# Decoder layer on one core: two of the seven products of the down-projection accumulated onto PSUM banks that were read before, and the first output rows finished by accumulating stores

## The chip, the core and the metric

The kernel runs on one core of a Trainium2 chip. Its engines are TensorE (PE, matrix products into eight banks of PSUM), VectorE (DVE), ScalarE (ACT), GpSimd (POOL) and SyncE (SP, which here only issues DMAs). PEld is the part of PE that loads the stationary operand of a matmul. The metric is the device time of one launch in microseconds (us); lower is better.

## The reference, cut to what matters

One decoder layer on a sequence of 512 tokens and 1024 channels in float32: two attention branches and their projections, then a gated MLP with a causal convolution of width 3. The attention part is not touched. The last lines are what the change works on:

```python
x = _layer_norm(DEEPNORM_ALPHA * x + (1.0 + gt1) * attn_out, ln1_g, ln1_b)
u2 = x * (1.0 + sc2) + sh2
h = _causal_depthwise_conv(u2 @ w_up, conv_w, conv_b)      # 1024 -> 2 x 2816
h_gate, h_val = jnp.split(h, 2, axis=-1)
ffn_out = (jax.nn.silu(h_gate) * h_val) @ w_down           # 2816 -> 1024
x = _layer_norm(DEEPNORM_ALPHA * x + (1.0 + gt2) * ffn_out, ln2_g, ln2_b)
```

`_layer_norm` subtracts the mean of a row, multiplies by the reciprocal of its standard deviation, multiplies by the row `ln2_g` and adds the row `ln2_b` (the offset row).

## The kernel before, in words

**Three matmuls for one product.** A float32 product is made of three matmuls on halves of reduced precision: high times high, high times low, low times high. Each weight that is loaded is therefore split: ACT copies it into the high half (`wh` or `wdh`, L182 for most), DVE subtracts that from the loaded weight (`wl` or `wdl`, L91). For activations the two halves lie in one tile `hv` (or `fh` and `fo`), 256 columns each.

**Loads.** SP issues the weight loads in a fixed order, that of a list of items (`add_item`, L956 to 1025). An item is a load into one of five raw buffers (`raw`, `LOADS = 5`) and the work on it, such as the split into one of three buffers (`WBUFS = 3`). `weights(k)` fetches item k and works off the ones before it. On PE, DVE, ACT and POOL the order of the program is only a wish: a scheduler places the instructions of each engine, which then run in the order that it set.

**Up-projection** (L1099 to 1145). 44 tiles of 128 hidden channels (n = 0 to 43), each of 24 matmuls into one PSUM bank, then convolution on ACT and DVE, SiLU on ACT, and the gate product on DVE. Two tiles make one of 22 gated tiles; two of these, `e` and `o`, make one of the 11 pairs (`FP = 11`, p = 0 to 10) of the down-projection.

**Down-projection.** For a pair, the 512 tokens are halved into rows blocks 0 and 1 above, 2 and 3 below, and the 1024 output columns into a left and a right half. So a pair is a product of 2 x 2 blocks with the weight blocks b11, b12, b21, b22 (128x512 each, stored in `wdp[p]` in the order b11, b12, b22, b21). It is done with seven block products in place of eight, each of them summed over the 11 pairs into two PSUM banks, one for each of its two row blocks:

- P1 (with b11), Y and Z2 run inside the up-projection and hold six banks (`yz`; `early_products`, L1087), for the last pair inside phase z.
- Z is phase z, with T3, a combination of two weight blocks; W1 is phase v, with T1, another one; X is phase x, with b21 as it is; W is phase w, with b22.

`blocks` (L1050) makes the combinations of activations (`g`, `s4`, and the changed `e`) on DVE. For the weights, `add_pair_items` loads b11 and b12 and adds b12 and b22 to them with an accumulating load of POOL, which gives the tile `b` with T1 in its left and T3 in its right half. `pair_proc` (L940 to 957) makes the two weights of Y and Z2 from b22 (L946) and b21 (L947), splits them, and stores `b` to a scratch tensor `t13[p]` and b22, multiplied by the gate row, to `wgt[p]`. The phases z, v and w load these again. The last pair (p = 10) has no such detour for `b`: it is split at once (`state["t13"]`).

**The gate row.** The channel gate multiplies the columns of the result (`g0` for the left, `g1` for the right half, both in `gt[1]`). In before, W alone has it in its weights (b22 is multiplied ahead); the other products are multiplied as results, in `gated` (L1155), one multiplication and one addition of 128x512 on DVE into the residual tile `r[i][e]` (row block i, half e; `xn` in the trace).

**The tail.** Phase x ends the row blocks 0 and 1: `first_rows` (L1226) makes their statistics and then `tail` (L1163): mean step (L1169), scaling and offset (L1173), store. Phase w has three pairs' weights loaded in its turn and the last eight (`LATE = 8`, `cli`) loaded early. For these eight, row block 2 is done in one piece of 512 columns into W's first bank and row block 3 in two pieces of 256 columns into fresh banks; then come subtraction or addition into `r`, statistics, `ln_stats` (L852) and `tail`, whose stores SP issues.

## Time and profile before

| what | value |
|---|---|
| three timed runs | 755.17, 755.78, 755.90 us, median 755.78 |
| the profiled execution | 754.3 us |
| its span (first to last instruction) | 752.5 us |
| granted clock of PE, mean | 0.995 |
| busy: PE, DVE, ACT, POOL | 98%, 81%, 51%, 14% of the span |
| read from and written to memory | 117.07 MB, 10.22 MB |

The profile is of one execution on the chip. A row of its timeline has the start of a group of alike instructions in us from the start of the span, the busy time of the group, the engine, the line of the program, the operation, what it writes and reads, and the count; in brackets, where the engine had stood idle before, how long, and which engine's work ended the wait. A row of the views of waits has the waiting engine and line, the work that released it, then the sum of the waits, their count and the longest.

### The profile page before, as it was taken

Reading aid. Unit: us, or ns where it says so; the run is one execution under the profiler, and the core shown is the slowest. Engines: PE = TensorE matmul, PEld = TensorE weight load, DVE = VectorE, ACT = ScalarE, POOL = GpSimd, SP = SyncE. Lnnn points to the kernel's source line nnn. Section 1 sums busy time; section 2 is a strip of 40 time slices with the busy share of each in tenths; the row PEclk is TensorE's granted clock in tenths of the full one; section 3 lists DMA queues with packets and bytes.
Section 4 is the critical chain, followed back from the end, with each engine's and each line's share of the span. In section 5 each row is a group of like instructions: output and inputs, shape, how many; then the busy total and the mean of one; then the engine's idle time right before and its main releaser. Section 6 shows DMA issues by size and latency. Waiting matters only on the chain.

```text
span 752.5 us, 9875 instructions
## 1 busy us (share of the span) xinstructions
PE 734.0 (98%) x3478; PEld 607.6 (81%) x3478; DVE 607.1 (81%) x1017; ACT 386.0 (51%) x678; POOL 109.0 (14%) x138
## 2 busy tenths in 40 slices
PE   8999999999999999999999999999999999999993
PEld 4878888878888888788889888888888888887883
DVE  6869799888788894765587889987696678769997
ACT  4566566685866564433065554454454355346530
POOL 1026223453010011453000000000000000000010
PEclk9999999999999999999999999999999999999997
DMA  8943446313422331542063778587874665557611
GB/s 331 405 175 116 164 169 214 122 58 112 169 92 83 108 112 62 195 168 84 1 240 77 252 243 275 161 250 223 253 213 165 187 218 151 171 182 264 220 63 57
DMA packets 43252, 128.01 MB, mean 170 GB/s; under 512 B 5665, under 2 KB 6177, under 8 KB 43202
## 3 DMA queue, kind: packets, MB, share of 16 engines
q1 hardware_dynamic: 37602, 112.09, 42.5%
q0 software_dynamic: 2576, 7.41, 5.2%
q10 hardware_dynamic: 3024, 7.88, 3.0%
q8 instruction: 27, 0.44, 0.2%
q14 instruction: 23, 0.19, 0.1%
HBM read 117.07 MB, written 10.22 MB: 169 GB/s over the span
## 4 chain that ended last, share of the span: by engine, by line
PE 82%; DVE 10%; DMA 3%; issue 2%; ACT 2%; POOL 0%; SPq 0%; DVEq 0%; ACTq 0%
PE ps L135 18%; PE ps L133 18%; PE ps L134 18%; PE ps L301 5%; PE ps L1077 3%; PE ps L1078 2%; PE ps L1076 2%; PE ps L552 2%; DVE wl L91 2%; PE ps L534 2%; PE ps L893 2%; PE ps L892 2%; PE ps L894 2%; PE ps L475 1%; PE ps L476 1%
## 5 line engine op out<-in xcount | busy, mean ns | idle before, releaser
L91 DVE TENSOR_TENSOR wl<-raw,wh 128x1024 fp32r<-128x1024 f32 (+2 forms) x112 | 139.2, 1244 | 53.9 <-ACT wh L182 53.5
L182 ACT ACTIVATE wh<-raw 128x1024 fp32r<-128x1024 f32 (+1 forms) x103 | 108.5, 1053 | 124.0 <-PE ps L134 59.8
L133 PE MATMUL ps<-u2h,wh 128*128 128x512 f32 (+1 forms) x376 | 141.6, 377 | 0.0
L135 PE MATMUL ps<-u2h,wl 128*128 128x512 f32 (+1 forms) x376 | 141.2, 376 | 0.0
L134 PE MATMUL ps<-u2l,wh 128*128 128x512 f32 (+1 forms) x376 | 141.2, 376 | 0.0
L133 PEld LDWEIGHTS ps<-u2h,wh 128*128 128x128 f32 x376 | 70.8, 188 | 13.6 <-issue 0.8
L135 PEld LDWEIGHTS ps<-u2h,wl 128*128 128x128 f32 x376 | 70.8, 188 | 12.8
L134 PEld LDWEIGHTS ps<-u2l,wh 128*128 128x128 f32 x376 | 70.8, 188 | 12.7
L133 PE MATMUL ps<-uh,wh 128*128 128x512 f32 x200 | 79.4, 397 | 0.0
L135 PE MATMUL ps<-uh,wl 128*128 128x512 f32 x200 | 78.3, 391 | 0.9 <-DVE wl L91 0.9
L134 PE MATMUL ps<-ul,wh 128*128 128x512 f32 x200 | 78.3, 391 | 0.0
L1124 ACT ACTIVATE cv<-ps,cw 128x512 f32<-128x512 f32 x44 | 33.9, 770 | 24.9 <-PE ps L135 19.0
L135 PEld LDWEIGHTS ps<-uh,wl 128*128 128x128 f32 x200 | 37.6, 188 | 9.5 <-DVE wl L91 1.3
L161 POOL DMA_DIRECT2D raw<-in_wdp x11 | 9.5, 867 | 244.1 <-DVE raw L947 95.0
L514 POOL TENSOR_TENSOR pt<-pt,om 128x127 f32<-128x127 f32 (+3 forms) x32 | 43.2, 1360 | 8.0 <-DVE om L513 8.0
L133 PEld LDWEIGHTS ps<-uh,wh 128*128 128x128 f32 x200 | 37.6, 188 | 7.4
L134 PEld LDWEIGHTS ps<-ul,wh 128*128 128x128 f32 x200 | 37.6, 188 | 7.2
L1125 DVE SCALAR_TENSOR_TENSOR cv<-ps,cw,cv 128x511 f32<-128x511 f32 x44 | 32.8, 745 | 9.1 <-ACT cv L1124 9.1
L1132 ACT ACTIVATE cv<-cv 128x512 f32<-128x512 f32 x22 | 13.9, 630 | 39.0 <-DVE cv L1126 38.9
L1126 DVE SCALAR_TENSOR_TENSOR cv<-ps,cw,cv 128x510 f32<-128x510 f32 x44 | 32.8, 745 | 0.2
L633 POOL TENSOR_TENSOR raw<-raw,gt 128x1024 f32<-128x1024 f32 x8 | 20.9, 2618 | 66.9 <-DMA raw<-in_wo 54.4
L513 DVE TENSOR_TENSOR_SCAN om<-om,dg 128x127 f32<-128x127 f32 (+3 forms) x32 | 29.6, 982 | 0.5 <-ACT om L508 0.4
(226 smaller groups left out, 1607.3 us busy)
## 6 DMA issues: line engine op xcount, KB each, us to landing
raw<-in_wup SPq DMA_DIRECT2D x44, 512.0 KB, 4.6
raw<-in_wa SPq DMA_DIRECT2D x32, 512.0 KB, 4.3
raw<-in_wct SPq DMA_DIRECT2D x25, 512.0 KB, 3.7
raw<-in_wdp SPq DMA_DIRECT2D x22, 512.0 KB, 5.7
wa<-in_wa SPq DMA_DIRECT2D x14, 512.0 KB, 7.9
raw<-in_wdp SPq DMA_DIRECT2D x22, 256.0 KB, 4.6
raw<-in_wdp POOLq DMA_DIRECT2D x11, 512.0 KB, 7.7
t<-raw ACTq DMA_DIRECT2D x10, 512.0 KB, 3.6
```

Of the source, the lines that this page charges most:

```text
L91: state["read"] = V.tensor_tensor(o, i, fl(hi), ALU.subtract)
L133: PE.matmul(ps, wh, ah, start=first, stop=False)
L134: PE.matmul(ps, wh, al, start=False, stop=False)
L135: return PE.matmul(ps, wl, ah, start=False, stop=last)
L182: state["hi"] = S.activation(h[:, 0:cols], r[:, 0:cols], AF.Copy)
L301: PE.matmul(grp[g], w, u, start=j == 0 and n == 0, stop=j == KT - 1 and n == (1 if g == 7 else 2))
L513: V.tensor_tensor_scan(d0, d0, dg[:, 513 - (e - s) : 512][:, ::-1], 0.0, ALU.mult, ALU.max)
L514: G.tensor_tensor(pt[b][:, s : e - 1], pt[b][:, s : e - 1], om[:, s + 1 : e], ALU.mult)
L1077: PE.matmul(ps, ah, bl, start=False, stop=False)
L1124: S.activation(t, ps, AF.Identity, bias=cw[:, n, 3:4], scale=cw[:, n, 2:3])
L1125: V.scalar_tensor_tensor(t[:, 1:], ps[:, 0:511], cw[:, n, 1:2], t[:, 1:], ALU.mult, ALU.add)
L1126: V.scalar_tensor_tensor(t[:, 2:], ps[:, 0:510], cw[:, n, 0:1], t[:, 2:], ALU.mult, ALU.add)
```

## The change

Seven things are changed, which hang together.

1. **T1 is multiplied by the gate row ahead** (`g1`, columns 512 to 1023 of `gt[1]`). For pairs 2 to 10, `pair_proc` does it on DVE before `b` is stored or split. For pairs 0 and 1, whose `b` is stored too early for that, two new items at up-tiles 23 and 27 load the T1 half of `t13[p]`, multiply it and store it back on POOL's queue (`scale_proc`).
2. **s4 changes its sign.** With it W1 + W, as gated sums, can be made by subtraction alone.
3. **X goes onto P1's two banks and W onto W1's two banks.** `product` and `phase` get a switch for it: the first matmul does not start the bank anew. No banks are taken for X and W, except the two 256-column pieces of row block 3 as before. P1 is read by DVE (through ACT's copy `p1`) before X begins; a bank of W1 is read before W's first matmul on it.
4. **The results are folded into `r` in another order.** Before: the four sums are built first and each is multiplied and added as a whole (`gated`). After: Y's, Z's and Z2's parts are folded as soon as they exist (`z_mark` 4 and 5, `v_mark` 2 to 5), W1 goes into `r[0][1]` and `r[1][1]` by one subtraction each (`x_mark`), P1 with X on it is multiplied straight from PSUM (`w_mark`), and W1 with W on it is subtracted at the end.
5. **The tail of row blocks 0 and 1 moves** with its statistics to `x_mark` 3 and 4 (`ROWS = (3, 4)`), the same phase steps as before, but each behind its subtraction of W1.
6. **Their output is filled ahead with the offset row:** two stores of 512 KB (128 rows each) from `lnr2[1]` on ACT's queue at up-tiles 30 and 32.
7. **They are finished by accumulating stores:** the mean step is done on DVE, the scaling with the row's reciprocal deviation on ACT in place of DVE's scaling and addition, and POOL issues the store with `accum_op=ALU.add`, which adds to what lies in the output.

The diff, cut to its core:

```diff
+ROWS = (3, 4)
...
             w = wdc_proc(r)
+            if p > 1:
+                V.tensor_tensor(b[:, 0:512], b[:, 0:512], gt[1][:, 512:1024], ALU.mult)
             with tc.issue_after(state["last"].ins):
...
+        if n in (23, 27):
+            t = t13[(23, 27).index(n)][:, 0:512]
+            add_item(t, scale_proc(t), 512)
...
-        V.tensor_tensor(s4, o[:, hi], e[:, lo], ALU.subtract)
+        V.tensor_tensor(s4, e[:, lo], o[:, hi], ALU.subtract)
...
+        if n in (30, 32):
+            S.dma_start(out[(n - 30) * 64 : (n - 30) * 64 + P, :], lnr2[1])
...
-                    product(ps[i], t[:, top[i]], t[:, bot[i]], *half(w, a), p == 0, p == FP - 1)
+                    product(ps[i], t[:, top[i]], t[:, bot[i]], *half(w, a), fresh and p == 0, p == FP - 1, not fresh)
...
             for i in range(2):
                 V.tensor_tensor(u2[i], p1[i], Y[i], ALU.subtract)
-                V.tensor_tensor(q1[i], u2[i], Z2[i], ALU.add)
+        if n in (4, 5):
+            fold(n - 2, 1, tm[n - 4], u2[n - 4], ALU.subtract)
...
-        if n == 0:
-            for i in range(2):
-                V.tensor_tensor(q1[i], q1[i], Z[i], ALU.add)
-                V.tensor_tensor(u3[i], u2[i], Z[i], ALU.add)
-        if n in (1, 2):
-            gated(n - 1, 0, q1[n - 1], q1[n - 1])
+        if n in (0, 1):
+            for a, b, c in zip((u3, q1)[n], (u2, u3)[n], (Z, Z2)[n]):
+                V.tensor_tensor(a, b, c, ALU.add)
+        if n in (2, 3):
+            fold(n - 2, 0, q1[n - 2], q1[n - 2])
+        if n in (4, 5):
+            fold(n - 4, 1, u3[n - 4], u3[n - 4], ALU.subtract)
...
-        tail(i, st, [(0, 0, 512), (1, 0, 512)], G)
+        tb = slice(i * P, (i + 1) * P)
+        mu, rs = ln_stats(st[:, 0:2, :])
+        for e in range(2):
+            c, v = slice(e * 512, (e + 1) * 512), r[i][e]
+            V.scalar_tensor_tensor(v, v, mu, lnr[0][:, c], ALU.subtract, ALU.mult)
+            S.activation(v, v, AF.Copy, scale=rs)
+            G.dma_start(out[tb, c], v, accum_op=ALU.add)
 
     def x_mark(n):
-        if n == 0:
-            for i in range(2):
-                V.tensor_tensor(c22[i], u3[i], W1[i], ALU.add)
-                V.tensor_tensor(u2[i], u2[i], W1[i], ALU.add)
-        if n in (1, 2):
-            gated(n - 1, 1, c22[n - 1], c22[n - 1], ALU.subtract)
-        if n in (3, 4):
-            first_rows(n - 3)
-        if n == 4:
-            for i in range(2):
-                gated(2 + i, 1, u2[i], u2[i], ALU.subtract)
-
+        if n in ROWS:
+            i = ROWS.index(n)
+            V.tensor_tensor(r[i][1], r[i][1], W1[i], ALU.subtract)
+            first_rows(i)
...
-    X = [bank() for _ in range(2)]
-    phase(X, xi, FP, lambda p: ops[p][1], x_mark)
-    W = [bank() for _ in range(2)]
+    phase(P1, xi, FP, lambda p: ops[p][1], x_mark, fresh=False)
...
-                V.tensor_tensor(p1[i], p1[i], X[i], ALU.add)
-                gated(2 + i, 0, p1[i], p1[i])
+                fold(2 + i, 0, p1[i], P1[i])
...
-                product(W[i], t[:, top[i]], t[:, bot[i]], *half(w, a), p == 0, i == 1 and p == FP - LATE - 1)
+                product(W1[i], t[:, top[i]], t[:, bot[i]], *half(w, a), False, i == 1 and p == FP - LATE - 1, True)
...
-    V.tensor_tensor(r[3][1], r[3][1], W[1], ALU.add)
+    V.tensor_tensor(r[3][1], r[3][1], W1[1], ALU.subtract)
...
-            V.tensor_tensor(v, v, ps, ALU.add)
+            V.tensor_tensor(v, v, ps, ALU.subtract)
```

The scheduler's order moves at three places. In the rows stand the line, the operation, the tile written and the tiles read (with buffer numbers), and the shape. The lines of after are six higher in the region of the product and one or some higher elsewhere.

On DVE, at the pair step of the last pair (p = 10, before L946 to 957): `raw_6255` (after: `raw_6273`) is the loaded b22 and b21, `raw_6217` (after: `raw_6235`) the tile `b` with T1 and T3, `gt_4554` the gate row, `wl` the low half of a weight of phase z, `hv` an activation's low half. Before:

```order
L946 TENSOR_TENSOR raw_6255<-raw_6255,raw_6217 128x512
L91 TENSOR_TENSOR wl_6460<-raw_6386,wh_6459 128x1024
L947 TENSOR_TENSOR raw_6255<-raw_6255 128x512
L91 TENSOR_TENSOR wdl_6371<-raw_6255,wdh_6369 128x512
L91 TENSOR_TENSOR wl_6490<-raw_6419,wh_6489 128x1024
L91 TENSOR_TENSOR wdl_6372<-raw_6255,wdh_6370 128x512
L91 TENSOR_TENSOR wdl_6380<-raw_6217,wdh_6378 128x512
L91 TENSOR_TENSOR wdl_6381<-raw_6217,wdh_6379 128x512
```

After:

```order
L947 TENSOR_TENSOR raw_6273<-raw_6273,raw_6235 128x512
L92 TENSOR_TENSOR wl_6479<-raw_6405,wh_6478 128x1024
L948 TENSOR_TENSOR raw_6273<-raw_6273 128x512
L92 TENSOR_TENSOR wdl_6389<-raw_6273,wdh_6387 128x512
L951 TENSOR_TENSOR raw_6235<-raw_6235,gt_4554 128x512
L92 TENSOR_TENSOR wdl_6390<-raw_6273,wdh_6388 128x512
L92 TENSOR_TENSOR wl_6507<-raw_6438,wh_6506 128x1024
L92 TENSOR_TENSOR wdl_6399<-raw_6235,wdh_6397 128x512
L92 TENSOR_TENSOR wdl_6400<-raw_6235,wdh_6398 128x512
L92 TENSOR_TENSOR hv_6432<-cv_6162,hv_6432 128x256
```

The scaling of T1 (L951) stands where a 1024-wide `wl` stood, and that `wl` comes one place later, behind the second `wdl`.

On PE, at the end of phase x and the start of phase w: `ps_6643` is a bank of X, `ps_6826` and `ps_6827` are W's banks for row blocks 2 and 3, `ps_6896` is the first 256-column piece of row block 3, `wl_6813` the low half of phase w's first weight. Before, the rows behind the last ones shown here are the other matmuls of the two 256-column pieces; the first 512-column low matmul comes when all 48 of them are done:

```order
L1078 MATMUL ps_6643<-wh_6776,hv_6416 128x512
L1076 MATMUL ps_6826<-wh_6812,hv_4191 128x512
L1076 MATMUL ps_6827<-wh_6812,hv_4191 128x512
L1076 MATMUL ps_6896<-wdh_6544,hv_4902 128x256
L1077 MATMUL ps_6896<-wdl_6545,hv_4902 128x256
L1078 MATMUL ps_6896<-wdh_6544,hv_4902 128x256
L1076 MATMUL ps_6896<-wdh_6588,hv_5128 128x256
```

After, `ps_4308` is a bank of P1, `ps_6538` and `ps_6539` are W1's banks, `ps_6905` is the 256-column piece and `wl_6826` the low half of phase w's first weight:

```order
L1084 MATMUL ps_4308<-wh_6792,hv_6435 128x512
L1082 MATMUL ps_6538<-wh_6825,hv_4191 128x512
L1082 MATMUL ps_6539<-wh_6825,hv_4191 128x512
L1082 MATMUL ps_6905<-wdh_6563,hv_4904 128x256
L1083 MATMUL ps_6905<-wdl_6564,hv_4904 128x256
L1084 MATMUL ps_6905<-wdh_6563,hv_4904 128x256
L1083 MATMUL ps_6538<-wl_6826,hv_4191 128x512
L1084 MATMUL ps_6538<-wh_6825,hv_4191 128x512
L1083 MATMUL ps_6539<-wl_6826,hv_4191 128x512
```

Three 256-column matmuls stand ahead of the first low one in place of 48; the other 45 now come last on PE, behind all of row block 2.

On DVE, from the end of row block 2 on: `xn_3625` and `xn_3626` are the two halves of row block 2, `xn_3742` is the right half of row block 3, `mv` the statistics, `ln_0` and `ln_1` the rows of the layer norm. Before:

```order
L1279 TENSOR_TENSOR xn_3742<-xn_3742,ps_6896 128x256
L1279 TENSOR_TENSOR xn_3742<-xn_3742,ps_6923 128x256
L1280 BN_STATS st_6829<-xn_3742 128x6 x2
L1279 TENSOR_TENSOR xn_3626<-xn_3626,ps_6826 128x512
L1280 BN_STATS st_6828<-xn_3626 128x6
L854 BN_AGGR mv_6883<-st_6828 128x2
L854 BN_AGGR mv_6950<-st_6829 128x2
```

After:

```order
L1284 TENSOR_TENSOR xn_3626<-xn_3626,ps_6538 128x512
...
L1284 TENSOR_TENSOR xn_3742<-xn_3742,ps_6905 128x256
L861 SCALAR_TENSOR_TENSOR mv_6892<-mv_6892 128x1
L1285 BN_STATS st_6840<-xn_3742 128x6
L1180 SCALAR_TENSOR_TENSOR xn_3625<-xn_3625,mv_6892,ln_1_5281 128x512
L1180 SCALAR_TENSOR_TENSOR xn_3626<-xn_3626,mv_6892,ln_1_5281 128x512
L1284 TENSOR_TENSOR xn_3742<-xn_3742,ps_6932 128x256
L1285 BN_STATS st_6840<-xn_3742 128x6
```

Row block 2 is now subtracted first and scaled (L1180) ahead of the last piece of row block 3; before, row block 3's right half was added first and both tails stood behind row block 2's last subtraction.

26 lines of the change are left out of this document (13 added, 13 removed).

## The prediction, on record before the result

> **What bounds the kernel now.** I read the page first: the share of each engine and the chain that ended last.
>
> ```profile
> span 752.5 us, 9875 instructions
> ...
> PE 734.0 (98%) x3478; PEld 607.6 (81%) x3478; DVE 607.1 (81%) x1017; ACT 386.0 (51%) x678; POOL 109.0 (14%) x138
> ...
> PE 82%; DVE 10%; DMA 3%; issue 2%; ACT 2%; POOL 0%; SPq 0%; DVEq 0%; ACTq 0%
> ```
>
> TensorE (PE) is busy nearly all the time, so a change that takes no matmul away can gain only where PE waits or where it has ended. The view by windows, cut at the stages that the change touches, shows where that is.
>
> ```profile
> core 0: us, PE busy (x) PEld busy (x) DVE busy (x) ACT busy (x) POOL busy (x), PEclk, DMA share, GB/s
> 560.00:665.00 105.00, 105.00 (x465) 86.92 (x464) 76.88 (x124) 45.99 (x75) 3.45 (x4) 1.00 0.62 187
> ...
> 681.00:692.00 11.00, 10.66 (x45) 7.91 (x44) 10.89 (x18) 7.95 (x16) 0.00 (x0) 1.00 0.66 221
> 692.00:724.50 32.50, 32.50 (x145) 26.92 (x144) 31.79 (x52) 17.89 (x26) 0.00 (x0) 1.00 0.52 177
> 724.50:741.00 16.50, 15.60 (x91) 13.51 (x89) 15.24 (x30) 0.29 (x1) 2.23 (x4) 1.00 0.17 64
> 741.00:752.50 11.50, 0.15 (x1) 0.00 (x0) 7.92 (x22) 0.48 (x2) 0.00 (x0) 0.65 0.25 92
> ```
>
> Up to 665 PE never rests and VectorE (DVE) has a quarter of its time free. From 681 on DVE is full (10.89 of 11.00, then 31.79 of 32.50). The last 11.5 us have no matmul: DVE finishes rows 2 and 3, then the output lands. PE's waits after 400 us, and ScalarE's (ACT) wait in the up-projection, are these rows of the views of waits:
>
> ```profile
> PEld ps L1077 <- DVE wdl L91: 1.2, 2, 0.7
> PEld ps L1077 <- DVE wl L91: 1.1, 1, 1.1
> ```
>
> ```profile
> ACT wh L182 <- PE ps L134: 33.0, 14, 5.0
> ```
>
> The 1.2 us lie in the last early products (687 to 690), the 1.1 us at the first split weight of phase w (731). ACT waits 14 times, up to 5.0 us, for PE to free a weight buffer: through the up-projection the weights are ahead of PE.
>
> **The up-projection: nothing.** Eleven DVE operations of 0.69 us are added (nine scalings of T1 in the pair step, two of the reloaded tiles), two 256 KB loads on SP's queue, two 256 KB stores on POOL's, two 512 KB stores of the offset row on ACT's. What hides them is the quarter of DVE that is free and the buffers that wait for PE. In the order each is placed beside work that waits already: the SP load of the first tile needs a slot that an early product before up-tile 19 frees, some eight tiles of the stream ahead; ACT's first fill stands behind the copy that waits for the layer-norm row today. If that cover were gone, a late weight costs PE its lateness beyond the reserve, up to 5.0 us. I take 0; the ends are 0 and 1 us.
>
> **The last pair product: +0.6 us.** Here DVE is full and PE waits for it. These are DVE's rows, then PE's weight loads.
>
> ```profile
> 687.00 0.68 DVE L91 TENSOR_TENSOR wdl<-raw,wdh 128x512 fp32r<-128x512 f32 x1
> 687.61 1.22 DVE L91 TENSOR_TENSOR wl<-raw,wh 128x1024 fp32r<-128x1024 f32 x1
> 688.74 1.89 DVE L91 TENSOR_TENSOR wdl<-raw,wdh 128x512 fp32r<-128x512 f32 x3
> 690.55 0.75 DVE L91 TENSOR_TENSOR hv<-cv,hv 128x256 fp32r<-128x256 f32 x2
> ```
>
> ```profile
> 689.48 0.19 PEld L1077 LDWEIGHTS ps<-wdl,fh 128*128 128x128 f32 x1 [0.52 <-DVE wdl L91]
> ...
> 691.02 0.19 PEld L1078 LDWEIGHTS ps<-wdh,hv 128*128 128x128 f32 x1
> ```
>
> The first fence of the section on the change shows the new scaling between the first and the second `wdl`, in place of a 1024-wide `wl`, which goes behind. Three 512-wide operations in a row take 1.89, so one occupies 0.60 of the queue and the `wl` 1.13 (687.61 to 688.74). The second `wdl` therefore starts at 688.21 and not 688.74, and PE loses its 0.52 us wait. But the `hv` at 690.55 gets later by the added 0.60, and PE stands at its low half already today (690.97 against the load at 691.02). So PE leaves this place 0.60 later; the earlier half microsecond is given back. Ends: 0 if the low half is not what holds it, 1.2 if ACT's splits, which now wait for the scaling, add as much again.
>
> **Phases z, v and x: DVE work, no time by itself.** From the first `u2` to the last fold the old order has 45 operations of 512 columns, the new one 35: six additions go because B21's products land on P1's banks and B22's on W1's, and four scalings go to ACT, which stands idle for 18 us at the end:
>
> ```profile
> 742.94 0.48 ACT L856 ACTIVATE mv<-mv,epsc 128x1 f32<-128x1 f32 x2 [18.15 <-DVE mv L854]
> ```
>
> PE does as many matmuls as before, with the same loads; that the first of a product accumulates too costs nothing by itself, since today the second and third do and PE shows no gap between them (145 matmuls fill 32.50 us, 0.224 each). PE is solid from 692 to 724.5, so all of this counts only where DVE meets PE again.
>
> **Phase w: -1.1 us and a new order.** PE's rows now, and the DVE and ACT rows that set its wait:
>
> ```profile
> 724.30 0.41 PEld L1076 LDWEIGHTS ps<-wh,hv 128*128 128x128 f32 x2
> ...
> 724.98 0.19 PEld L1077 LDWEIGHTS ps<-wdl,hv 128*128 128x128 f32 x1
> ...
> 730.49 0.19 PEld L1078 LDWEIGHTS ps<-wdh,hv 128*128 128x128 f32 x1
> 731.78 0.19 PEld L1077 LDWEIGHTS ps<-wl,hv 128*128 128x128 f32 x1 [1.10 <-DVE wl L91]
> ...
> 740.54 0.19 PEld L1078 LDWEIGHTS ps<-wdh,hv 128*128 128x128 f32 x1
> ```
>
> ```profile
> 715.20 1.06 ACT L182 ACTIVATE wh<-raw 128x1024 fp32r<-128x1024 f32 x1 [1.14 <-PE ps L1078]
> ```
>
> ```profile
> 719.03 1.28 DVE L1229 BATCH_NORM_STATS2 st<-xn 128x6 f32<-128x512 f32 x2
> ...
> 722.88 0.69 DVE L1229 BATCH_NORM_STATS2 st<-xn 128x6 f32<-128x512 f32 x1
> ...
> 730.51 1.22 DVE L91 TENSOR_TENSOR wl<-raw,wh 128x1024 fp32r<-128x1024 f32 x1
> ```
>
> Today PE does the 48 matmuls of 256 columns (row block 3) first, 0.12 us each (46 steps in 5.51 us), because the `wl` of phase w stands behind 11.5 us of DVE work (719.03 to 730.51); it still waits 1.10 us, then does the 512-wide ones, 0.225 each. After, 45 of the 48 come last. When is `wl` there? DVE's work for rows 0 begins behind the split of x's fifth weight, which ACT starts at 715.20 when PE frees a buffer, so at 715.80 with the 0.60 from above; 1.06 on ACT and 1.13 on DVE bring it to 718.1. Ahead of `wl` then stand two subtractions of W1, four statistics, two short splits (eight times 0.60), two mean steps of 0.66 and some 0.5 us of small ones: 6.6 us, so `wl` runs from 724.7 to 725.9. PE ends x at 724.90, has two hi matmuls (0.45) and three small ones (0.36) and wants `wl` at 725.7. It waits about 0.15 us; ends 0 and 1.1. PE's last load: 740.54 + 0.60 - 1.10 + 0.15 = 740.2.
>
> A new wait goes with the banks: PE's first matmul onto W1 of rows 1 must wait for DVE's subtraction from that bank, on which the rest of PE's queue then hangs. In the sum above the subtraction ends at 723.3, and today's statistics of rows 1 start at 722.88; PE wants the bank at 725.1, so 1.8 us are in hand and I take 0. On this the Trainium skill, Perfetto Trace Analysis, section Optimizing Tensor Performance, has a rule against the change: independent matmul groups should rotate through PSUM banks, so that an evacuation overlaps the next group. By the rows the sum gets 0 from it; by the rule PE would stand for the evacuation. No run so far shows the case; it is the slower rival below.
>
> **After the last matmul: -3.5 us.** DVE's rows, SP's stores, and the price of 256-wide operations:
>
> ```profile
> 738.36 0.75 DVE L1279 TENSOR_TENSOR xn<-xn,ps 128x256 f32<-128x256 f32 x2
> 739.02 0.75 DVE L1280 BATCH_NORM_STATS2 st<-xn 128x6 f32<-128x256 f32 x2
> 741.19 0.69 DVE L1279 TENSOR_TENSOR xn<-xn,ps 128x512 f32<-128x512 f32 x1 [1.42 <-PE ps L1078]
> ...
> 742.64 0.31 DVE L854 BATCH_NORM_AGGREGATE mv<-st 128x2 f32<-128x12 f32 x2
> ...
> 744.46 0.15 DVE L857 TENSOR_SCALAR mv<-mv 128x1 f32<-128x1 f32 x1
> ...
> 744.66 0.75 DVE L1169 SCALAR_TENSOR_TENSOR xn<-xn,mv,ln 128x512 f32<-128x512 f32 x1
> 745.32 1.41 DVE L1173 SCALAR_TENSOR_TENSOR xn<-xn,mv,ln 128x512 f32<-128x512 f32 x2
> ...
> 747.64 1.54 DVE L1173 SCALAR_TENSOR_TENSOR xn<-xn,mv,ln 128x512 f32<-128x512 f32 x3
> ```
>
> ```profile
> 746.10 3.62 SPq L1174 DMA_DIRECT2D out<-xn  x5
> ```
>
> Today both row blocks' tails stand behind PE: 741.19 to 749.18, 8.0 us. After, rows 2 end first on PE and their tail lies beside the 45 small matmuls. For rows 3 alone remain: half of 0.75 to subtract, half of 0.75 for statistics, 0.24 to aggregate, 744.66 to 749.18 without the two scalings of rows 2 (4.52 - 1.33 = 3.2), and 0.3 for a reciprocal and the gaps between dependent ones: 4.5 us. Does the tail of rows 2 fit? Its last matmul loads 45 times 0.12 before 740.2, at 734.8; DVE starts 0.65 later (as 740.54 to 741.19), needs 3.27 (741.19 to 744.46), then 0.75 for the first half of rows 3 and 1.33 to scale: 740.8. The last piece is there at 740.2 + 0.55 = 740.75. It just fits, without reserve. DVE ends at 740.75 + 4.5 = 745.25, against 749.18. The last store takes what it takes today, 3.3 us to 752.5.
>
> The accumulating stores of rows 0 and 1 are new. DVE and ACT have rows 1 ready at about 729. What such a store takes lies between these two rows, the plain store and the accumulating load of twice the size:
>
> ```profile
> out<-xn POOLq DMA_DIRECT2D x4, 256.0 KB, 2.4
> ...
> raw<-in_wdp POOLq DMA_DIRECT2D x11, 512.0 KB, 7.7
> ```
>
> By either it ends before 738, far ahead of the end: 0.
>
> **Sum.** +0.60 - 1.10 + 0.15 - 3.5 - 0.1 (a 256-wide matmul ends sooner after its load) = -3.9 us. The profiled execution took 754.3 (span 752.5 and 1.8 around it), so 750.4 on its terms; the median of the three runs, 755.78, stands 1.5 above it, and there the forecast is 751.9. Without the 0.60 and the 0.15 it is 751.1; with 1.2 and 1.1 in their place 753.5.
>
> **Rivals.** First, **DVE is late by 1 to 2.5 us** in x or in the tail of rows 2, for which nothing is in hand: each microsecond there is one at the end, 753 to 754.3. For it speaks DVE's 98% from 692 on, against it that ten operations leave that stretch. Second, **the tail does not shrink**: were rows 2 finished only with rows 3, the 8.0 us stay and only the PE part remains, 755.4. Against it speaks DVE's order, in which the whole tail of rows 2 stands ahead of the last piece. Third, **slower: PE stands before W1's banks and `wl`**. Today 48 small matmuls cover DVE's lateness; after, three do. If DVE reached `wl` when it does today, at 730.51 and not 724.7, PE would idle 5.8 us more: 757.7. It costs from 0.2 us of lateness on and turns the sign at 3.9. For it speaks that row, against it that the four scalings and three of the fold operations that stood before `wl` are gone from there. By the page's rule on banks this is the expected case.
>
> **Chances.** Forecast 0.66, DVE a little late 0.15, tail unchanged 0.08, slower 0.11. A measurement of this kernel tells 0.2% (1.5 us) from no change, so faster means below 754.3: 0.66 + 0.15 = 0.81; the same 0.08; slower 0.11. The range goes from 750.8 (the low end of the sum and 0.3 for the runs) to 754.3, the first rival's end, and leaves out 0.19.
>
> **What would show it.** Right: the wait at the first `wl` of phase w under 0.3 us and the small matmuls last on PE; DVE's last scaling about 4.5 us after its last subtraction starts; the load at 691.02 now near 691.6; rows 0 and 1 landed before 740. Wrong: PE waits for `wl` or for a subtraction for more than 1 us near 725; a scaling of rows 2 behind the last subtraction; PE waits between 400 and 665; or an accumulating store among the last landings.

## The result and the profile after

The changed kernel takes 750.74 us (median of 6 runs, 750.24 to 751.83) against 755.47 (6 runs, 754.58 to 756.43): a ratio of 0.994, 95% interval 0.9927 to 0.9953. As a time, 750.74 lies 0.06 us below the low end of the forecast range, 750.8. The range was laid out from a median of 755.78 for the kernel before; at that median the ratio of 0.994 is 751.2, inside it. Beside the last experiments the changed kernel was timed again: median 750.44 (5 runs) against 754.95 (10 runs), ratio 0.9939 (0.9925 to 0.9952). Of all runs here four took much longer (921.79 to 4180.81 us, of three different kernels) and are left out of every median. The profiled execution took 750.47 us with a span of 748.7; before it was 754.3 with 752.5.

First the page of after: the span, the busy times, and the chain that ended last.

```profile
span 748.7 us, 9890 instructions
...
PE 734.3 (98%) x3478; PEld 608.1 (81%) x3478; DVE 607.9 (81%) x1018; ACT 389.0 (52%) x682; POOL 111.1 (15%) x140
...
PE 86%; DVE 7%; DMA 3%; ACT 2%; issue 2%; POOL 0%; SPq 0%; DVEq 0%; ACTq 0%
```

PE is as busy as before (734.3 against 734.0 us), DVE too (607.9 against 607.1). In the chain DVE's share fell from 10% to 7% and PE's rose from 82% to 86%; where two paths are nearly tied the chain follows one of them, so these shares say where to look and not how much was gained. The windows at the same stages:

```profile
core 0: us, PE busy (x) PEld busy (x) DVE busy (x) ACT busy (x) POOL busy (x), PEclk, DMA share, GB/s
560.00:665.00 105.00, 105.00 (x464) 86.90 (x463) 80.83 (x130) 47.15 (x76) 4.87 (x6) 1.00 0.63 193
681.00:692.00 11.00, 10.15 (x43) 7.44 (x41) 10.49 (x16) 8.10 (x15) 0.00 (x0) 1.00 0.61 201
692.00:724.50 32.50, 32.49 (x143) 26.88 (x144) 32.17 (x54) 17.68 (x25) 0.00 (x0) 1.00 0.55 186
724.50:741.00 16.50, 16.46 (x96) 14.40 (x94) 13.43 (x31) 3.68 (x7) 3.51 (x4) 1.00 0.48 64
741.00:748.70 7.70, 0.00 (x0) 0.00 (x0) 4.49 (x14) 0.29 (x1) 0.00 (x0) 0.83 0.38 137
```

In the up-projection DVE has 4 us more to do and PE still never rests. From 681 to 692 PE is busy for 10.15 in place of 10.66: half a microsecond is lost there, behind 0.39 us that PE had lost just before (followed up in the part on the prediction). From 724.5 to 741 it is busy for 16.46 in place of 15.60. Behind 741 stand 7.7 us in place of 11.5. The weight loads of PE at the three places of the prediction:

```profile
688.13 0.19 PEld L1083 LDWEIGHTS ps<-wdl,fh 128*128 128x128 f32 x1 [0.67 <-DVE wdl L92]
...
692.01 0.19 PEld L1084 LDWEIGHTS ps<-wdh,hv 128*128 128x128 f32 x1 [1.06 <-DVE hv L92]
...
726.20 0.19 PEld L1083 LDWEIGHTS ps<-wl,hv 128*128 128x128 f32 x1
...
740.56 0.19 PEld L1084 LDWEIGHTS ps<-wdh,hv 128*128 128x128 f32 x1
```

The wait of 0.52 for the second `wdl` is gone and one of 1.06 for the low half `hv` is new; the wait of 1.10 for `wl` is gone (no bracket at 726.20); the last load comes at 740.56, as before (740.54). And DVE's rows around that `wl` and at the end:

```profile
722.94 0.67 DVE L1249 TENSOR_TENSOR xn<-xn,ps 128x512 f32<-128x512 f32 x1
...
724.92 1.21 DVE L92 TENSOR_TENSOR wl<-raw,wh 128x1024 fp32r<-128x1024 f32 x1
...
735.61 0.69 DVE L1284 TENSOR_TENSOR xn<-xn,ps 128x512 f32<-128x512 f32 x1 [2.97 <-PE ps L1084]
...
739.68 1.40 DVE L1180 SCALAR_TENSOR_TENSOR xn<-xn,mv,ln 128x512 f32<-128x512 f32 x2
741.00 0.42 DVE L1284 TENSOR_TENSOR xn<-xn,ps 128x256 f32<-128x256 f32 x1
...
744.08 1.54 DVE L1180 SCALAR_TENSOR_TENSOR xn<-xn,mv,ln 128x512 f32<-128x512 f32 x3
```

`wl` runs from 724.92 to 726.13, and PE loads it at 726.20: a tie. Row block 2's subtraction starts at 735.61 and its scaling (739.68) ends at about 741.0, when the last piece of row block 3 is there too. From that piece's subtraction to DVE's end are 4.6 us (741.00 to 745.62); before, 8.0 us stood behind PE.

### The profile page after: what moved, and what is told of

The parts are those of the page before. It is cut to its first block, busy times and chain, and to the rows that moved or that the text cites. A ratio compares the mean times of both kernels' runs of the same rounds, so it can differ in the third digit from the quotient of the medians.

```text
span 748.7 us, 9890 instructions
## 1 busy us (share of the span) xinstructions
PE 734.3 (98%) x3478; PEld 608.1 (81%) x3478; DVE 607.9 (81%) x1018; ACT 389.0 (52%) x682; POOL 111.1 (15%) x140
## 4 chain that ended last, share of the span: by engine, by line
PE 86%; DVE 7%; DMA 3%; ACT 2%; issue 2%; POOL 0%; SPq 0%; DVEq 0%; ACTq 0%
PE ps L136 18%; PE ps L134 18%; PE ps L135 18%; PE ps L302 5%; PE ps L1084 4%; PE ps L1082 4%; PE ps L1083 4%; PE ps L553 2%; PE ps L535 2%; PE ps L895 2%; PE ps L893 2%; PE ps L894 2%; DVE wl L92 1%; PE ps L476 1%; PE ps L477 1%
## 5 line engine op out<-in xcount | busy, mean ns | idle before, releaser
L1134 DVE SCALAR_TENSOR_TENSOR cv<-ps,cw,cv 128x510 f32<-128x510 f32 x44 | 32.7, 743 | 0.3
```

What stands on the lines that cost most here:

```text
L1134: V.scalar_tensor_tensor(t[:, 2:], ps[:, 0:510], cw[:, n, 0:1], t[:, 2:], ALU.mult, ALU.add)
```

## The experiments

Each ran in 5 rounds against the kernel before on the same chip. Beside the ratio I use one measure inside each profile that is free of what happened earlier in it: the time from PE's last load to DVE's end (740.54 to 749.18 in before, 8.6 us; 740.56 to 745.62 in after, 5.1). A second one, for the whole of the stages that the change touches, stands in a table at the end of this section. Many of the intervals of the ratios overlap with that of the changed kernel, so the ratios alone often do not decide between two expectations; then the rows do.

**The two halves apart.** The first kernel leaves the fill and the accumulating stores away:

```diff
-        if n in (30, 32):
-            S.dma_start(out[(n - 30) * 64 : (n - 30) * 64 + P, :], lnr2[1])
...
-            S.activation(v, v, AF.Copy, scale=rs)
-            G.dma_start(out[tb, c], v, accum_op=ALU.add)
+        tail(i, st, [(0, 0, 512), (1, 0, 512)], G)
```

> The changed kernel without the fill of the output and without accumulating stores: the rows 0 to 255 are scaled and offset on VectorE and stored as in before; the accumulation onto read PSUM banks and the scaled T1 stay. My theory: the four scalings (0.66 us each) come back to VectorE, two of them ahead of the first low half of phase w, which is then ready 1.3 us later. TensorE covers that with 12 more of the 256-column matmuls (15 in place of 3 stand ahead in the order), so it does not wait, but row block 2 ends 1.4 us later and VectorE's 10.0 us of work behind it (735.61 to 745.62) move with it: +1.4 us on the changed kernel, about 752.1 us (a ratio of 0.9955 to before). Rival A, the stores carry most of the gain: 754 us or more. Rival B, the stores carry none of it: 750.7 us.

Measured: ratio 0.9953 (0.9941 to 0.9966), median 751.68. DVE's rows at its end:

```profile
737.01 0.69 DVE L1276 TENSOR_TENSOR xn<-xn,ps 128x512 f32<-128x512 f32 x1 [1.75 <-PE ps L1084]
...
742.33 0.41 DVE L1276 TENSOR_TENSOR xn<-xn,ps 128x256 f32<-128x256 f32 x1
...
745.41 1.54 DVE L1178 SCALAR_TENSOR_TENSOR xn<-xn,mv,ln 128x512 f32<-128x512 f32 x3
```

Row block 2's subtraction starts 1.40 us later than in after (737.01 against 735.61), and DVE ends 1.33 later (746.95); the last piece now waits for DVE (742.33), not DVE for it. That is my theory's size. Rival A is out by the time. The interval overlaps with the changed kernel's (0.9927 to 0.9953), so against rival B it is these rows that speak, 1.3 to 1.4 us.

The second adds the fill and the accumulating stores to the kernel before, with the same lines the other way round.

> The kernel before with the fill and the accumulating stores of rows 0 to 255 alone; X and W keep their own banks, T1 is not scaled. My theory: four scalings leave VectorE ahead of the first low half of phase w, which starts at 727.9 us and not at 730.5; the order has 35 of the 48 small matmuls ahead of it (4.2 us), so TensorE's wait of 1.1 us goes and 13 small ones come last. Row block 2's last subtraction starts at 738.7 in place of 741.2 and has 8.0 us and the second piece's 0.75 behind it: VectorE ends at 747.5 in place of 749.2, -1.7 us on before, a ratio of 0.9977 (753.8 us). Rival A, the parts only work together: within 0.3 us of before. Rival B, the stores carry most: -3 us or more.

Measured: ratio 0.9975 (0.9966 to 0.9985), median 752.96, in the profile:

```profile
747.88 1.54 DVE L1175 SCALAR_TENSOR_TENSOR xn<-xn,mv,ln 128x512 f32<-128x512 f32 x3
```

```profile
741.51 0.19 PEld L1078 LDWEIGHTS ps<-wdh,hv 128*128 128x128 f32 x1
```

This profiled execution was late as a whole (754.4 us, against a median of 752.96), so only its inner distances are read: from PE's last load to DVE's end are 7.9 us in place of 8.6. The ratio is the one expected. So the stores alone bring 0.25%, the rest of the change alone 0.47%, both 0.6%. The two parts add up to 0.12% more than both together, which is less than the width of the intervals: whether a part of the gain is the same one, the times do not show.

**The order on TensorE.** The changed kernel with the small matmuls first again: the products of the two pieces are traced ahead of phase w, and phase w's are tied behind them.

```diff
+    small = [bank()[:, 0:256] for _ in range(2)]
...
+            m = product(small[n], t[:, top[1]], t[:, bot[1]], ...)
...
+                with tc.issue_after(m.ins):
+                    product(W1[i], t[:, top[i]], t[:, bot[i]], *half(w, a), False, ...)
```

> The changed kernel with TensorE's old order at the end: both 256-column pieces of row block 3 (48 matmuls) run ahead of phase w's 512-column ones. Nothing else is changed. My theory: TensorE ends when it does now (last load 740.6), but the tails of row blocks 2 and 3 both stand behind it again, 8.0 us in place of 4.9: +3.3 us on the changed kernel, about 754.0 us (ratio 0.998). Rival, the gain is VectorE's lighter work and not the order on TensorE: 750.7 us, no difference to the changed kernel.

Measured: ratio 0.9994 (0.9984 to 1.0003), median 754.55. In its profile PE's last load stands at the same time as in after, and DVE does both tails behind it:

```profile
741.21 0.69 DVE L1290 TENSOR_TENSOR xn<-xn,ps 128x512 f32<-128x512 f32 x1 [3.31 <-PE ps L1084]
...
742.66 0.31 DVE L855 BATCH_NORM_AGGREGATE mv<-st 128x2 f32<-128x12 f32 x2
...
747.66 1.53 DVE L1180 SCALAR_TENSOR_TENSOR xn<-xn,mv,ln 128x512 f32<-128x512 f32 x3
```

Every operation of the change is still there, and nearly the whole gain is gone. The `x2` at 742.66 is the sign: the statistics of row blocks 2 and 3 are aggregated together. The end moved from 745.62 to 749.19, 3.6 us.

The reverse: the kernel before with the small matmuls forced last.

```diff
+                    if i:
+                        es.enter_context(tc.issue_after(m2.ins))
```

> The kernel before with the order of the changed one forced on TensorE at the end: all 48 matmuls of 256 columns (row block 3) behind row block 2's. Nothing else is changed. My theory: the order alone does not bring the gain, since VectorE still reaches the first low half of phase w at 730.5: TensorE then waits from about 724.9 to 731.7, has 8.8 us for row block 2 and 5.8 for the small ones, and its last load comes at about 746.3; with 0.55 and VectorE's 4.5 behind it VectorE ends at 751.3 in place of 749.2: +2.2 us on before, a ratio of 1.003. Rival, the order alone brings the gain of the tail: -3.5 us on before, a ratio of 0.995.

Measured: ratio 1.0059 (1.0045 to 1.0073), median 759.14, 4.4 us slower than before, twice what I had worked out. The load and the windows around it:

```profile
724.42 0.19 PEld L1077 LDWEIGHTS ps<-wl,hv 128*128 128x128 f32 x1
724.64 0.19 PEld L1078 LDWEIGHTS ps<-wh,hv 128*128 128x128 f32 x1
...
732.23 0.29 PEld L1077 LDWEIGHTS ps<-wl,hv 128*128 128x128 f32 x1 [6.95 <-DVE wl L91]
...
732.83 0.33 PEld L1077 LDWEIGHTS ps<-wl,hv 128*128 128x128 f32 x1
733.26 0.33 PEld L1078 LDWEIGHTS ps<-wh,hv 128*128 128x128 f32 x1
```

```profile
core 0: us, PE busy (x) PEld busy (x) DVE busy (x) ACT busy (x) POOL busy (x), PEclk, DMA share, GB/s
724.50:732.00 7.50, 1.21 (x6) 0.67 (x4) 7.50 (x18) 0.41 (x2) 2.23 (x4) 0.77 0.35 134
732.00:733.00 1.00, 0.77 (x2) 0.67 (x3) 1.00 (x3) 0.00 (x0) 0.00 (x0) 0.50 0.12 45
733.00:734.00 1.00, 1.00 (x4) 0.81 (x3) 1.00 (x3) 0.00 (x0) 0.00 (x0) 0.50 0.00 0
...
735.00:736.00 1.00, 1.00 (x5) 0.82 (x4) 1.00 (x3) 0.00 (x0) 0.00 (x0) 0.78 0.00 0
736.00:740.00 4.00, 4.00 (x20) 3.27 (x19) 2.77 (x5) 0.00 (x0) 0.00 (x0) 1.00 0.00 0
```

The wait of 6.95 is about the one expected. What I had left out is the column PEclk: after the wait the granted clock is 0.50, in the window from 735 to 736 it turns to 1.00 (0.78 on average), and meanwhile the loads come every 0.43 us (732.83 to 733.26) in place of 0.22 (724.42 to 724.64). At twice the time for each, the 3.2 us from 732.2 to about 735.4 held 1.6 us of extra time. The clock had fallen at about 728.6 (1.00 from 728 to 728.5, 0.61 from 728.5 to 729, 0.50 after), some 2.9 us after PE's last matmul. The Trainium skill, TensorE: Matmul & The Clock Gate, section Part 1: The HAM clock gate, says that the clock falls to half after an idle window of some 3.4 us and returns after as long a time of work; this trace shows both steps, a little sooner, after 2.9 and 3.2 us. Some 0.5 us of the miss is not the edit's: in this profile PE was already 0.5 us late when phase z went on to its next bank (678.86 against 678.35). The order alone is no gain; it becomes one only when `wl` is early.

**The reserve at the first low half of phase w.** Three more operations on DVE ahead of it, whose result is not used:

```diff
+            if i == 1:
+                for _ in range(3):
+                    dm.append(V.tensor_tensor(tm[0], r[2][0], g0, ALU.mult))
...
+        with tc.issue_after(dm[-1].ins):
+            w = weights(k)
```

> The changed kernel with three more VectorE operations of 512 columns (1.8 us, their result is not used) ahead of row block 1's subtraction and of the first low half of phase w. The order then has 18 small matmuls ahead of that half in place of 3. My theory: there is no reserve (the low half ends at 726.13, TensorE loads it at 726.20), so all of it is paid: no wait on TensorE, but row block 2 ends 1.8 us later and so does everything behind it, +1.8 us on the changed kernel, about 752.5 us. Rival, the small matmuls that move ahead cover it and the tail has reserve: +0.5 us or less.

Measured: ratio 0.9957 (0.9944 to 0.9969), median 751.62. The three rows are `wl`, row block 2's subtraction and DVE's last operation:

```profile
727.23 1.20 DVE L92 TENSOR_TENSOR wl<-raw,wh 128x1024 fp32r<-128x1024 f32 x1
...
737.90 1.14 DVE L1290 TENSOR_TENSOR xn<-xn,ps 128x512 f32<-128x512 f32 x2 [2.97 <-PE ps L1084]
...
745.97 1.54 DVE L1180 SCALAR_TENSOR_TENSOR xn<-xn,mv,ln 128x512 f32<-128x512 f32 x3
```

`wl` is 2.3 us later than in after, PE does not wait (18 small matmuls stand ahead), and DVE ends at 747.51, 1.9 later. But 0.5 us of both is not the edit's: in this profile PE was that late already at 679.24, where it stood at 678.74 in after. So `wl` and row block 2 show all of the 1.8 us added, and the end shows 1.4 of it; the medians differ by 0.9 to 1.2. The theory holds up to row block 2; behind it some 0.4 us are made up, which it had not foreseen. The rival's +0.5 is out by the rows; the ratios' intervals overlap.

**W on fresh banks.**

```diff
+    W = [bank() for _ in range(2)]
+    for i in range(2):
+        V.tensor_tensor(r[2 + i][1], r[2 + i][1], W1[i], ALU.subtract)
```

> The changed kernel with W on two fresh PSUM banks: W1 of row blocks 2 and 3 is subtracted by two more VectorE operations (0.6 us each), and no matmul goes onto a bank that VectorE has just read. My theory: the bank cost nothing (no wait stands at TensorE's first matmuls on it) and the two operations fall into VectorE's idle 2.97 us ahead of row block 2's end: within 0.5 us of the changed kernel, 750.7 us. Rival, the rule that groups should rotate through banks: faster by at least 0.7 us, the time of one subtraction that TensorE would otherwise stand for.

Measured: ratio 0.993 (0.9916 to 0.9944), median 750.03. That is 0.7 us below the changed kernel's first median, the rival's size, but the intervals overlap (0.9927 to 0.9953), so the times decide nothing here. The two more subtractions stand together, and behind them DVE still waits for row block 2:

```profile
729.13 1.28 DVE L1261 TENSOR_TENSOR xn<-xn,ps 128x512 f32<-128x512 f32 x2
...
736.36 0.69 DVE L1287 TENSOR_TENSOR xn<-xn,ps 128x512 f32<-128x512 f32 x1 [1.77 <-PE ps L1084]
```

DVE's idle time there shrank from 2.97 to 1.77, by the two operations. Against the rival speak the traces: in after PE has no wait at its first matmuls on W1's banks, so there is nothing for fresh banks to save, and in the table below the two kernels are equal (66.90 and 66.88). So accumulating onto a bank that was read some 2 us before neither cost nor brought anything in phase w; what it saved on DVE there lay in idle time.

**The last pair's T1.** First, its scaling on GpSimd in place.

```diff
-                V.tensor_tensor(b[:, 0:512], b[:, 0:512], gt[1][:, 512:1024], ALU.mult)
+                (G if p == FP - 1 else V).tensor_tensor(b[:, 0:512], b[:, 0:512], gt[1][:, 512:1024], ALU.mult)
```

> The changed kernel with one operation on another engine: T1 of the last pair is scaled by GpSimd in place of VectorE. My theory: the low half that TensorE waits for at 692.0 comes 0.60 us earlier, -0.5 us on the changed kernel, about 750.2 us. Rival A, ScalarE and VectorE now wait for GpSimd's slower operation (1.3 us by its 2.56 for twice the columns) and the gain is lost: 750.7 us or 0.7 more. Rival B, the wait has another cause: 750.7 us.

Then on GpSimd into a tile of its own, split later:

```diff
+                G.tensor_tensor(state["t1"], b[:, 0:512], gt[1][:, 512:1024], ALU.mult)
...
+        if n == 5:
+            h, l = z(F32R, "wdh"), z(F32R, "wdl")
+            hi_of(h, state["t1"])
+            lo_of(l, state["t1"], h)
```

> The changed kernel, but for the last pair T1 is scaled by GpSimd into a tile of its own and split at the last step of phase z, not in the pair step; VectorE loses the scaling (0.60) and moves one split (0.60) away from the place where TensorE waits 1.06 us for a low half (hv) at 692.0. My theory: most of this wait goes; the split comes back in phase z, where VectorE is full, so the first low half of phase w may be late by 0.3: -0.75 us on the changed kernel (-0.4 to -1.0), about 750.0 us. Rival A, the wait is set by ScalarE's splits and not by VectorE's queue: 750.7 us. Rival B, GpSimd's work slows VectorE down: 750.7 us or more.

Measured: 0.9966 (0.9954 to 0.9979), 752.27 us, for the first, and 0.9952 (0.994 to 0.9965), 750.91 us, for the second: no gain, and the first loses about 1.5 us (more than rival A's 0.7). The same GpSimd operation in the two kernels, first in place, then early into its own tile:

```profile
686.02 5.13 POOL L951 TENSOR_TENSOR raw<-raw,gt 128x512 f32<-128x512 f32 x1 [29.81 <-DVE raw L947]
```

```profile
680.99 1.30 POOL L959 TENSOR_TENSOR t<-raw,gt 128x512 f32<-128x512 f32 x1 [24.48 <-PE ps L1089]
```

And the DVE operation that ran beside the second:

```profile
681.29 2.08 DVE L92 TENSOR_TENSOR wl<-raw,wh 128x1024 fp32r<-128x1024 f32 x1 [0.60 <-ACT wh L183]
```

My expectation fell: it is rival A for the first kernel and rival B for the second. Beside a DVE without pause the operation took 5.13 us in place of 1.30, and ScalarE's splits waited for it (2.85 us). In that kernel DVE's last operation before its next pause is this one, and GpSimd's ended (691.15) 1.15 us behind its end (690.00), about the time that it takes by itself, which fits a GpSimd that stood until DVE paused:

```profile
689.32 0.68 DVE L92 TENSOR_TENSOR wdl<-raw,wdh 128x512 fp32r<-128x512 f32 x1
691.84 0.69 DVE L92 TENSOR_TENSOR wdl<-raw,wdh 128x512 fp32r<-128x512 f32 x1 [1.84 <-ACT wdh L649]
```

In the other kernel, where GpSimd started first (680.99), DVE's 1024-wide `wl` took 2.08 in place of 1.22; taking 0.60 off DVE cost it 0.86. The Trainium skill, SBUF — State Buffer, section Who interferes with whom, says that a VectorE instruction with two inputs in SBUF contends with a GpSimd instruction that reads SBUF for a shared port, that the port is locked, and that the order of issue decides which of them waits; both rows agree, and in the first GpSimd's 3.8 us of extra time span several VectorE instructions. Since this spoilt the test, I ran it without GpSimd: ScalarE copies T1, and DVE's scaling and split of it are written at the end of phase z.

```diff
+                S.activation(state["t1"], b[:, 0:512], AF.Copy)
...
+        if n == 5:
+            V.tensor_tensor(state["t1"], state["t1"], g1, ALU.mult)
```

> The changed kernel, but for the last pair ScalarE copies T1 into a tile of its own, and VectorE scales and splits it at the last step of phase z, not in the pair step: 1.2 us of VectorE leave the place where TensorE waits 1.06 us at 692.0, and GpSimd does nothing. My theory: this wait goes, a wait of 0.5 for the second early weight comes back as in before, so TensorE leaves the place 0.5 us earlier; but the 1.2 us come back on VectorE in phase z, where it is full until the first low half of phase w (724.92), which then stays where it is. The order puts 6 small matmuls ahead of it in place of 3, and row block 2 gains little: -0.2 us on the changed kernel (-0.5 to 0). Rival, VectorE's place in the pair step was no bound: 0 or slower by the copy (0.6).

> The changed kernel once more, beside the next three on the same chip, as their base. A ratio of 0.994 to before again (0.9927 to 0.9953); if the profiled execution alone were right (750.47 against 754.3), 0.995.

Measured: 0.9943 (0.9931 to 0.9955), 750.64 us, beside 0.9939 and 750.44 for the changed kernel, which repeats its first ratio: no difference. PE's loads at the place, DVE's scaling of T1, and its `wl` of phase w:

```profile
690.03 0.19 PEld L1088 LDWEIGHTS ps<-wdl,fh 128*128 128x128 f32 x1 [0.51 <-DVE wdl L92]
...
691.57 0.19 PEld L1089 LDWEIGHTS ps<-wdh,hv 128*128 128x128 f32 x1
```

```profile
689.89 0.68 DVE L1225 TENSOR_TENSOR t<-t,gt 128x512 f32<-128x512 f32 x1
...
724.82 1.20 DVE L92 TENSOR_TENSOR wl<-raw,wh 128x1024 fp32r<-128x1024 f32 x1
```

The edit did less than its description says. The scheduler placed the scaling (L1225) in the pair step all the same, behind the second `wdl`; only one split of 0.60 us left it. Still the wait of 1.06 is gone, the one of 0.51 is back, and `wl` stays about where it was (724.82 against 724.92), since the split came back ahead of it. From the load at which phase z goes on to its next bank to this load of the pair step are 12.67 us in before (678.35 to 691.02), 13.27 in after (678.74 to 692.01) and 12.68 here (678.89 to 691.57). So one operation of 0.60 us more or less for DVE ahead of `hv` is 0.60 us more or less for PE there, and the scaling of T1 was one more; but taking one away helps only if `wl` comes earlier too. That is the last pair of kernels: row block 1's subtraction and tail traced behind the first weight of phase w, alone and with the edit above.

```diff
         w = weights(k)
+        if n == 0:
+            x_mark(9)
```

> The changed kernel with row block 1's subtraction of W1, its statistics and its tail traced behind the first weight of phase w, so that VectorE makes this low half before the two statistics (1.2 us earlier) and no small matmul stands ahead of it on TensorE. My theory: TensorE did not wait there, so it ends as before (last load 740.6) and the last piece still sets the end: 0 to -0.2 us on the changed kernel. Rival, VectorE's 10 us behind row block 2 set the end: -0.36 us, as row block 2 ends three small matmuls earlier.

> The last two edits together. My theory: now the 0.5 us that TensorE leaves the pair step earlier reach the end, since the low half of phase w is there in time: -0.5 us on the changed kernel (-0.2 to -0.9), about 0.9933 of before. Rival, something else holds the end (VectorE's chain or the last store): 0.

Measured: 0.9939 (0.9926 to 0.9951), 750.02 us, alone, and 0.9934 (0.9922 to 0.9946), 749.98 us, together. Against 0.9939 the first is no change, as expected. The second is 0.46 us below the changed kernel by the medians, with intervals that overlap, and hardly below the 750.02 and 750.03 of two other kernels: not shown to be faster by the times. Its profile has both effects, `wl` at 723.29 and DVE's end 0.67 us earlier than in after (744.95), of which 0.15 it had gained before:

```profile
723.29 1.23 DVE L92 TENSOR_TENSOR wl<-raw,wh 128x1024 fp32r<-128x1024 f32 x1
...
743.41 1.54 DVE L1185 SCALAR_TENSOR_TENSOR xn<-xn,mv,ln 128x512 f32<-128x512 f32 x3
```

**One distance for all.** The profiled executions differ by up to two microseconds before the last stages begin, which blurs every comparison of their ends. The table takes that out: it has the load at which phase z goes on to its next bank (the one with `issue` in its bracket, 678.74 in after), DVE's end, and the time between. What is lost ahead of that load, such as after's 0.39 us, is not in it.

| kernel | load | DVE's end | between |
|---|---|---|---|
| before | 678.35 | 749.18 | 70.83 |
| before with the stores alone | 680.23 | 749.42 | 69.19 |
| before with the small matmuls last | 678.86 | 753.51 | 74.65 |
| after | 678.74 | 745.62 | 66.88 |
| after once more | 679.10 | 745.95 | 66.85 |
| no fill, no accumulating stores | 678.72 | 746.95 | 68.23 |
| small matmuls first | 678.98 | 749.19 | 70.21 |
| three more operations | 679.24 | 747.51 | 68.27 |
| W on fresh banks | 679.48 | 746.38 | 66.90 |
| T1 scaled on GpSimd in place | 678.91 | 747.10 | 68.19 |
| T1 on GpSimd, own tile | 678.49 | 745.67 | 67.18 |
| T1 copied by ScalarE | 678.89 | 745.83 | 66.94 |
| `wl` first | 678.24 | 745.09 | 66.85 |
| the last two together | 678.59 | 744.95 | 66.36 |

Each row but after's is a single execution; after's two agree to 0.03. The change is worth 3.95 us by this measure. Where the ratios left something open, it speaks for the expectations: without the fill and the accumulating stores it is 1.35 us less (expected 1.4), the stores alone bring 1.64 (expected 1.7), the old order on PE takes back 3.3 (expected 3.3), W on fresh banks changes nothing (0.02), and the last two edits together bring 0.52 more (expected 0.5), while each of them alone brings nothing. The kernel before with the small matmuls last loses 3.8 us, the 2.2 expected and the 1.6 of the half clock.

## Why the prediction was right, point by point

**What bounds the kernel** held: the time follows DVE from the pair step of the last pair on, and the end follows from when `wl` of phase w is there (in the kernel with three more operations it was later by the 1.8 us added, and the end by 1.4, with the 0.5 us that PE was late ahead of it taken off).

**Up-projection, nothing:** right up to 665, where PE is busy for 105.00 of 105.00 us from 560 on in both. Behind it 0.39 us were lost, as the next point shows; the end of this term had been put at 1 us.

**Last pair, +0.60:** right in size and cause. The load that stood at 691.02 was expected near 691.6 and stands at 692.01, but 0.39 of that PE had lost before the pair step. The loads at which phase z begins on its next bank show it: 678.35 in before, 678.74 in after, with a wait of 0.78 in place of 0.51.

```profile
678.74 0.19 PEld L1082 LDWEIGHTS ps<-wh,hv 128*128 128x128 f32 x1 [0.78 <-issue]
```

```profile
PE ps L1082 <- DVE cv L1134: 0.4, 1, 0.4
```

This 0.4 us was not in the sum; 0.12 of it PE has lost before this load (677.77 against 677.65 for the one ahead). The matmul's own wait (the second fence) points to the last convolution, DVE's L1134, which reads a bank of the up-projection. Followed further back, it begins with a load from memory: ACT's split of a reloaded weight waits for its DMA, and runs 0.82 us later in after. First before, then after:

```profile
668.08 1.06 ACT L182 ACTIVATE wh<-raw 128x1024 fp32r<-128x1024 f32 x1 [1.04 <-DMA raw<-t]
```

```profile
668.90 1.06 ACT L183 ACTIVATE wh<-raw 128x1024 fp32r<-128x1024 f32 x1 [1.42 <-DMA raw<-t]
```

Behind it in ACT's order stands the first step of a convolution (670.17 against 669.35), and DVE's steps of the convolutions follow from there. In the kernel with `wl` first this split starts at 668.38, and the wait is 0.51 as in before; in the other kernels with the change it starts at 668.64 or later, and the wait is 0.78 to 0.91. Why the load lands later is not shown. One candidate is the change itself: the last `b` that goes to the scratch tensor is now scaled first, and its store is issued at 660.41 in place of 659.75, just ahead of these loads.

**Phases z, v, x:** right. PE has no wait from 692 to 724.5.

**Phase w, -1.10 and +0.15:** right. DVE reached `wl` at 724.92 (forecast 724.7; the terms of that sum give 718.0 where it says 718.1, which changes nothing). The 0.15 did not come, because PE was late by the same 0.4; that one lateness hid the other is luck. W1's bank was free in time: its subtraction ran from 722.94 to 723.61, some 2 us before PE's second matmul of phase w. On rotating through banks, the rule of the Trainium skill's Perfetto Trace Analysis, section Optimizing Tensor Performance, had PE stand there in the prediction's third rival; the trace shows no wait, and the kernel with fresh banks shows no gain in the table. By this trace the rule does not bind when the evacuation ends some 2 us before the bank is wanted.

**Behind the last matmul, -3.5:** right: 4.6 us from the last piece's subtraction to DVE's end (forecast 4.5), the end at 745.62 (745.25). The kernel with the small matmuls first shows that this is the order's doing: 3.3 us of it come back by the table, 3.6 by the time from PE's last load to DVE's end. The tail of row block 2 fits with nothing to spare, as forecast.

**The accumulating stores, 0:** right. They took 5.5 us to landing (the median of four), between the two rows that bounded them (2.4 and 7.7):

```profile
out<-xn POOLq DMA_DIRECT2D x4, 256.0 KB, 5.5
```

```profile
729.51 1.75 POOL L1244 DMA_DIRECT2D out<-xn  x2 [1.81 <-ACT xn L1243]
```

POOL has issued the last by 731.3, so at the median it lands by about 737; the longest of all stores to the output took 7.2, which would still be before 740.

**The sum** on the profiled execution was 750.4; it took 750.47. The stages that the change touches gave 3.95 us, as worked out. That the whole agrees to 0.07 is in part luck: DVE's end came 0.37 later than forecast (745.62 against 745.25), from the 0.39 lost ahead of the pair step, and the span ended 3.1 us behind it in place of 3.3; and the six runs differ among themselves by 1.6 us. **The number that was off is the step to the median.** I put the median 1.5 us above the profiled execution, because the three runs shown were (755.78 against 754.3). In the later runs of the kernel before the medians were 754.57 (19 runs), 754.77 (9) and 754.95 (10), 0.3 to 0.7 above it. After's median of 750.74 stands 0.3 above its profiled execution, and the second one, 750.44, 0.4 below its own (750.84). So 751.9 was 1.2 too high, and the time lies at the low end of the range, by 0.06 us below it. With an offset of 0.5 the forecast would have been 750.9.

**The slower rival** had the right mechanism and too low a price: 5.8 us of waiting were priced at 5.8. The kernel with such a wait (6.95 us) shows some 1.6 us more for the half clock behind it. And in the kernels whose order was left free, the later `wl` was, the more small matmuls stood ahead of it (3 in after, 15 without the fill, 18 with three more operations, 35 in before with the stores alone), so that lateness was paid in the tail and not as a wait.

## What to carry to other kernels

When one engine is busy to the end, look at what stands behind its last instruction, and put the pieces with the shortest work behind them last; here that order was worth 3.3 of the 3.95 us that the change gained in its stages, but only because another engine's queue had been made light enough to feed it. Work taken from a full queue counts only if everything in that queue up to the next meeting point gets earlier: moving an operation a little further along the same queue gave nothing here. Before comparing the ends of two profiles, find a point ahead of the stages in question that both have, and measure from there. Take the offset between the profiled execution and the median from more than three runs.

## What the runs showed of the hardware

- In a wait of 6.95 us PE's granted clock fell to 0.50 some 2.9 us after the last matmul; it stayed there for the first 3.2 us of work behind the wait, and the 512-column matmuls came every 0.43 us in place of 0.22. Waits of about 1 us left the clock at 1.00.
- GpSimd and VectorE held each other up, each way in one execution. The same 128x512 multiplication took 1.30 or 5.13 us on GpSimd, and a 128x1024 subtraction on VectorE 2.08 in place of 1.22 beside it.
- A 256 KB store took 5.5 us to landing when it accumulated, against 2.4 for the plain ones on the same queue in before (medians of four).
- Matmuls that accumulate onto a bank that VectorE had finished reading some 2 us before came every 0.23 us like all the others, with no wait at the first one.
